# A two-layer decoder trunk on one core: reordering the chain of its post-norms and moving small operations between engines

## The chip, the core and the metric

The kernel runs on one core of a Trainium2 chip. The metric is the device time of one execution, in microseconds (us); less is better. Engines are named as in the profile: PE is TensorE (matrix products and 128x128 transposes), DVE is VectorE, ACT is ScalarE, POOL is GpSimd, SP is SyncE, which issues most DMAs.

## What is computed

The input is x, 512 tokens by 1024 channels in float32, and one condition vector c. Two layers follow each other; each has two sub-layers and each sub-layer ends in a post-norm. Cut to what matters here:

```python
for l in range(2):
    mod = silu(c) @ ada_w[l] + ada_b[l]          # 6 x 1024: shift, scale, gate, twice
    shift1, scale1, gate1, shift2, scale2, gate2 = split(mod, 6)
    h = x * (1 + scale1) + shift1
    a, u, v = split(h @ w_in[l])                 # 512 columns each
    y_a = pool_mixer(a, pool_w[l], pool_scale[l])         # windows 2, 4, 8, 16
    y_b = gelu(u) * (tril(sgu_w[l]) @ norm(gelu(v)) + sgu_b[l])
    x = layernorm(alpha * x + gate1 * (concat(y_a, y_b) @ w_out[l])) * ln1_g + ln1_b
    h = x * (1 + scale2) + shift2
    g, val = split(h @ w_up[l])                  # 2816 columns each
    f = (gelu(causal_conv3(g)) * val) @ w_down[l]
    x = layernorm(alpha * x + gate2 * f) * ln2_g + ln2_b
```

## The kernel before, in words

Every product is made of three float32r matmuls (high part by high part, high by low, low by high), so each weight tile is loaded by SP, cast to its high part `whi` on ACT (L178) and its low part `wlo` is subtracted on DVE (L181). The order of the work on every engine is the order of the program text; nothing is rescheduled. Generators stand for pieces of work that the text weaves between others (`weave`), and counters say how many weight tiles are loaded, split and ready; at most four stand ready at a norm.

Tokens lie in four chunks of 128 (`NCH`). The residual `xr[c]` is one tile of 128 tokens by 1024 channels for each chunk. A sub-layer ends in two projections, one for each half of the channels. `project` makes the first half for all chunks (banks `ps0`). Then `project_and_norm` (L404) goes chunk by chunk: the second half on PE (`n_pj`), on DVE the gated residual of that half (`residual`, L339 and L341 or L343), `bn_stats` of both halves (L428), `bn_aggr` (L320), on POOL the eps (L322) and the power -0.5 (L323), on DVE the normalisation in place (L434), on PE eight transposes of the normalised chunk (`turn`, L349), on ACT the affine map of the next sub-layer by columns (L361) and the high part `hh` (L363), on DVE the low part `hl` (L364). PE's order is: second half of chunk 0, of chunk 1, transposes of 0, second half of chunk 2, transposes of 1, second half of chunk 3, transposes of 2. `after_norm` (L483) goes on with four weight tiles of the next product over chunks 0 and 1; between its second and its third tile stand the transposes of chunk 3; then come the same four tiles over chunks 2 and 3. The low parts of up to four weight tiles are split around chunk 3: one ahead of its second half, the others behind its `bn_aggr`.

This chain occurs three times: behind the mixer of layer 0 (the first norm), behind the MLP of layer 0 (the second), behind the mixer of layer 1 (the third). The last norm, at the end, is `project_and_end` (L440), which shares `rstd_of` (L318). The residual of the following sub-layer is `xr * (alpha*g) + alpha*b`: ACT scales the rows g and b as soon as they are loaded (L378) and POOL computes it on whole chunks (`next_residuals`, L367).

The small loads of the mixer of layer 0 (`poolw`, `wst`, `sb`), the counts `rcnt`, the columns of layer 1 and four loads for the gating norm are issued by POOL at the very start (L227 to L233), on a DMA queue of its own. During layer 0 DVE also sums the modulation products (`ada_sum`, L243), a 128x1024 operation for each 512 KB of `ada_w`; the ones that the first norm needs end right ahead of it.

## Time and profile before

| what | value |
|---|---|
| time, median of 3 runs | 1016.14 us (1015.49 to 1018.05) |
| time of the profiled execution | 1017.41 us |
| its span, first to last instruction | 1015.7 us |
| PE busy | 986.6 us, 97% of the span |
| DVE busy | 648.1 us, 64% |
| ACT busy | 364.1 us, 36% |
| POOL busy | 108.5 us, 11% |

The profiled execution took 1.71 us more than its span, and 1.27 us more than the median. PE is busy nearly throughout, so the time is PE's work plus the holes in it. A row of a timeline gives the start of an instruction in us from the start of the span, its duration, engine, line, operation, what it writes and reads, its shape, and in brackets the idle time in front of it with what ended it. A row of a table by stretches gives the busy time of each engine, then the granted clock of PE (1.00 is 2.4 GHz, 0.50 is 1.2 GHz), the busy share of the 16 DMA engines and what they moved.

### The profile page before, as it was taken

To read this page: it belongs to the slowest core of one execution; us is meant where nothing else is said; L and a number is where in the kernel's file an instruction comes from. 1 tells how busy PE (TensorE), PEld (TensorE's weight loads), DVE (VectorE), ACT (ScalarE), POOL (GpSimd) and SP (SyncE) were. 2 spreads that over 40 slices of the span, in tenths; PEclk is the share of its full clock that TensorE was granted. 3 is DMA by queue.
4 is the path that set the end of the run, shared out by engine and by line. 5 is a ranking of instruction groups with operands and counts; after the bars stand their busy time and mean duration, and the time that the engine had idled before them with its cause. 6 is when DMAs were issued, how large, how long until landed. Compare 5 with 4: busy or idle time off the path is not lost.

```text
span 1015.7 us, 11993 instructions
## 1 busy us (share of the span) xinstructions
PE 986.6 (97%) x4691; PEld 826.9 (81%) x4691; DVE 648.1 (64%) x907; ACT 364.1 (36%) x532; POOL 108.5 (11%) x89
## 2 busy tenths in 40 slices
PE   6999979999999999999999999999999999999996
PEld 5788768888888888888888878888888888888885
DVE  5979986868644376585699455877544245444456
ACT  3553264443322233333263432733433213333300
POOL 2010028000000000000064100540000000000002
PEclk9999999999999999999999999999999999999999
DMA  9979514767632355476115221355323332323302
GB/s 323 406 296 352 194 57 145 245 198 243 193 121 86 142 182 191 154 242 207 42 63 181 100 69 36 104 197 179 121 87 101 104 104 83 103 86 102 125 1 83
DMA packets 43849, 153.55 MB, mean 151 GB/s; under 512 B 5152, under 2 KB 5312, under 8 KB 43792
## 3 DMA queue, kind: packets, MB, share of 16 engines
q1 hardware_dynamic: 43344, 151.89, 43.6%
q0 software_dynamic: 448, 0.89, 0.3%
q8 instruction: 37, 0.61, 0.3%
q14 instruction: 20, 0.16, 0.1%
HBM read 150.67 MB, written 2.10 MB: 150 GB/s over the span
## 4 chain that ended last, share of the span: by engine, by line
PE 83%; DVE 9%; DMA 3%; ACT 3%; issue 1%; POOL 1%; SPq 0%; DVEq 0%; POOLq 0%; ACTq 0%
PE up L217 15%; PE up L218 15%; PE up L216 15%; PE down L387 6%; PE down L388 6%; PE down L389 6%; DVE wlo L181 2%; PE n_pj L388 1%; PE n_pj L389 1%; PE n_pj L387 1%; DMA ada<-in_ada_w_dram 1%; PE v L580 1%; PE a L580 1%; DMA raw_w_in<-in_w_in_dram 1%; ACT ht_n L361 1%
## 5 line engine op out<-in xcount | busy, mean ns | idle before, releaser
L218 PE MATMUL up<-hh,wlo 128*128 128x512 f32 (+1 forms) x768 | 285.9, 372 | 2.4 <-DVE wlo L181 2.4
L217 PE MATMUL up<-hl,whi 128*128 128x512 f32 (+1 forms) x768 | 285.9, 372 | 1.8 <-DVE hl L364 1.8
L216 PE MATMUL up<-hh,whi 128*128 128x512 f32 (+1 forms) x768 | 286.6, 373 | 0.0
L181 DVE TENSOR_TENSOR wlo<-raw_w_up,whi 128x1024 fp32r<-128x1024 f32 x88 | 118.7, 1353 | 143.8 <-ACT whi L178 143.8
L218 PEld LDWEIGHTS up<-hh,wlo 128*128 128x128 f32 x768 | 145.2, 189 | 27.7 <-DVE wlo L181 2.8
L217 PEld LDWEIGHTS up<-hl,whi 128*128 128x128 f32 x768 | 145.3, 189 | 26.9 <-DVE hl L364 2.2
L216 PEld LDWEIGHTS up<-hh,whi 128*128 128x128 f32 x768 | 145.4, 189 | 25.0
L181 DVE TENSOR_TENSOR wlo<-raw_w_down,whi 128x1024 fp32r<-128x1024 f32 x44 | 53.9, 1225 | 114.9 <-ACT whi L178 113.3
L178 ACT CAST whi<-raw_w_up 128x1024 fp32r<-128x1024 f32 x88 | 90.9, 1045 | 57.0 <-PE down L389 52.6
L387 PE MATMUL down<-whi,gh 128*128 128x512 f32 x272 | 105.8, 389 | 0.0
L388 PE MATMUL down<-wlo,gh 128*128 128x512 f32 x272 | 105.8, 389 | 0.0
L389 PE MATMUL down<-whi,gl 128*128 128x512 f32 x272 | 105.8, 389 | 0.0
L243 DVE SCALAR_TENSOR_TENSOR ada<-ada,c 128x1024 f32<-128x1024 f32 x68 | 82.6, 1217 | 4.4 <-DMA ada<-in_ada_w_dram 4.4
L828 ACT ACTIVATE y<-y 128x512 f32<-128x512 f32 x44 | 27.9, 634 | 143.2 <-DVE y L825 143.2
L178 ACT CAST whi<-raw_w_down 128x1024 fp32r<-128x1024 f32 x44 | 46.1, 1048 | 80.6 <-PE down L389 80.6
L818 ACT ACTIVATE y<-up,cols 128x512 f32<-128x512 f32 x44 | 34.3, 779 | 89.5 <-PE up L218 87.9
L389 PEld LDWEIGHTS down<-whi,gl 128*128 128x128 f32 x272 | 51.1, 188 | 10.7
L387 PEld LDWEIGHTS down<-whi,gh 128*128 128x128 f32 x272 | 51.0, 188 | 10.6
L388 PEld LDWEIGHTS down<-wlo,gh 128*128 128x128 f32 x272 | 51.0, 188 | 10.6
L322 POOL TENSOR_SCALAR rs_n<-mv_n 128x1 f32<-128x1 f32 x12 | 7.2, 600 | 480.7 <-DVE mv_n L320 480.7
L361 ACT ACTIVATE ht_n<-tr_n,B,A 128x128 f32<-128x128 f32 x96 | 36.0, 454 | 60.1 <-PE tr_n L349 60.1
L181 DVE TENSOR_TENSOR wlo<-raw_w_in,whi 128x1024 fp32r<-128x1024 f32 (+1 forms) x26 | 37.8, 1477 | 10.0 <-ACT whi L178 9.9
(170 smaller groups left out, 1459.6 us busy)
## 6 DMA issues: line engine op xcount, KB each, us to landing
raw_w_up<-in_w_up_dram SPq DMA_DIRECT2D x88, 512.0 KB, 3.3
ada<-in_ada_w_dram SPq DMA_DIRECT2D x68, 512.0 KB, 4.2
raw_w_down<-in_w_down_dram SPq DMA_DIRECT2D x44, 512.0 KB, 3.2
raw_w_in<-in_w_in_dram SPq DMA_DIRECT2D x24, 512.0 KB, 5.5
raw_w_out<-in_w_out_dram SPq DMA_DIRECT2D x16, 512.0 KB, 4.5
xr<-in_ada_w_dram SPq DMA_DIRECT2D x12, 512.0 KB, 9.9
lent<-in_ada_w_dram SPq DMA_DIRECT2D x8, 512.0 KB, 9.9
lent_h<-in_ada_w_dram SPq DMA_DIRECT2D x8, 512.0 KB, 7.6
```

The lines of the kernel that those rows point to most:

```text
L178: A.copy(hi, src)
L181: (eng or V).tensor_tensor(lo, src, hi.bitcast(F32), op=ALU.subtract)
L216: T.matmul(ps, w[0], x[0], start=start, stop=False)
L217: T.matmul(ps, w[0], x[1], start=False, stop=False)
L218: T.matmul(ps, w[1], x[0], start=False, stop=stop)
L243: V.scalar_tensor_tensor(raw, raw, 0.5, c2, op0=ALU.mult, op1=ALU.mult, accum_out=modc[l][:, o : o + 1])
L361: A.activation(tmp[:, w], ps[hf][:, w], AF.Identity, bias=cb[:, k : k + 1], scale=ca[:, k : k + 1])
L387: T.matmul(ps[:, f], ah[:, cs], wh, start=i + j == 0, stop=False)
L388: T.matmul(ps[:, f], ah[:, cs], wl, start=False, stop=False)
L389: T.matmul(ps[:, f], al[:, cs], wh, start=False, stop=i + j == n - 1)
L818: A.activation(y, pg, AF.Identity, bias=col[:, C_CB + j : C_CB + j + 1], scale=col[:, cw + 2 : cw + 3])
L828: A.activation(y, y, AF.Gelu_apprx_tanh)
```

## The change

- The norm's chain: the first halves of chunks 0 and 1 (residual and statistics) come ahead of the loop, that of chunk c + 2 between the statistics and the normalisation of chunk c. The statistics of a half follow its residual at once. The low parts `hl` of chunk c - 1 come behind the normalisation of chunk c. Of the weight tiles split at chunk 3 two come ahead of its second half, one between its statistics and its normalisation, a fourth (in the first norm) behind.
- eps is added on DVE, the power stays on POOL.
- The next residuals are computed on DVE, one 128x1024 operation behind each pair of an MLP or each weight tile of the mixer, instead of on POOL; 8 operations behind each of the three norms.
- ACT scales the rows g and b behind the first two pairs of the MLP, not ahead of the last chunk's affine map.
- The nine small loads go to SP: `rcnt` behind the second group of first loads, the others behind five more modulation sums, where the mixer of layer 0 begins. `z_bias` of layer 0 moves behind `pool_group(3)`.

```diff
-    poolw, wst, sb = mix_loads(0, G)
-    G.dma_start(rcnt, a["rcnt"])
-    G.dma_start(cols[1], a["cols"][1])
...
+    def first_mix_loads():
+        tiles = mix_loads(0)
...
+                    nc.sync.dma_start(t[:, i, :], a[n][i].rearrange("(h d) -> d h", h=4))
+        nc.sync.dma_start(cols[1], a["cols"][1])
+        return tiles
...
-        G.tensor_scalar(rs, mv[:, 1:2], EPS, None, op0=ALU.add)
+        V.tensor_scalar(rs, mv[:, 1:2], EPS, None, op0=ALU.add)
         G.tensor_tensor(rs, rs, neg_half, op=ALU.pow)
...
     def next_residuals(grow, brow):
+
         for c in range(NCH):
-            G.tensor_tensor(xr[c], xr[c], grow, op=ALU.mult)
-            G.tensor_tensor(xr[c], xr[c], brow, op=ALU.add)
...
+            for row, op in ((grow, ALU.mult), (brow, ALU.add)):
+                later.append(lambda c=c, row=row, op=op: V.tensor_tensor(xr[c], xr[c], row, op=op))
+
+    def one_later():
+        if later:
+            later.pop(0)()
...
+        half(ps0[0], 0, 0)
+        half(ps0[1], 1, 0)
         for c in range(NCH):
...
             if c == NCH - 1:
-                refill(4 - len(ready), None, lows)
-                for f in lows[:1]:
-                    f()
-            before = None
-            if c:
-                before = modulate(c - 1, turn(c - 1, tag), tag, AB)
-            residual(ps, c, 1, gate, scale=scale)
-            for hf in range(2):
-                V.bn_stats(sts[c][:, hf, :], xr[c][:, halves(hf)])
+                split(2)
+            before = modulate(c - 1, turn(c - 1, tag), tag, AB) if c else None
+            half(ps, c, 1)
             mv, rs = rstd_of(sts[c], f"{tag}{c}")
-            for f in lows[1:]:
-                f()
-            if before:
-                next(before)
+            if c + 2 < NCH:
+                half(ps0[c + 2], c + 2, 0)
+            elif c == NCH - 1:
+                split(1)
             V.tensor_scalar(xr[c], xr[c], mv[:, 0:1], rs, op0=ALU.subtract, op1=ALU.mult)
             if before:
-                next(before)
-            if c + 1 < NCH:
-                residual(ps0[c + 1], c + 1, 0, gate, scale=scale)
+                weave([before])
+            if c == NCH - 1:
+                split(4)
...
+        if k == 1:
+            nc.sync.dma_start(rcnt, a["rcnt"])
...
-            pump(MIX_FILL[0], fill)
+            pump(MIX_FILL[0] - 1, fill)
+            poolw, wst, sb = first_mix_loads()
+            lower_triangles()
+            pump(1, fill)
...
                 weave([pair(0, *up[:2]), pair(1, *up[2:])], side * 4)
+                scaled((grow, brow))
...
                 weave([pair(j, *up)], side * 2)
                 j += 1
+                one_later()
```

Here `half` is `residual` and then `bn_stats` of one half, `split(n)` splits up to n weight tiles until four are ready, and `scaled` is ACT's scaling of the rows.

DVE at the start of the first norm, before: from the first half of chunk 0 (`res_0`, `xr_84`) to its normalisation by L434 and the first half of chunk 1 (`xr_85`).

```order
L339 TENSOR_TENSOR res_0_1058<-out_0_0_905,gate_2_722 128x512
L343 SCALAR_TENSOR_TENSOR xr_84<-xr_84,res_0_1058 128x512
L339 TENSOR_TENSOR res_1_1086<-n_0_pj_0_1061,gate_2_722 128x512
L343 SCALAR_TENSOR_TENSOR xr_84<-xr_84,res_1_1086 128x512
L428 BN_STATS stn_0_0_1054<-xr_84 128x6 x2
L320 BN_AGGR mv_n_0_0_1091<-stn_0_0_1054 128x2
L434 TENSOR_SCALAR xr_84<-xr_84,mv_n_0_0_1091,rs_n_0_0_1093 128x1024
L339 TENSOR_TENSOR res_0_1097<-out_0_1_906,gate_2_722 128x512
```

The same place now (the normalisation is L450; `xr_86` is chunk 2).

```order
L426 BN_STATS stn_0_0_1054<-xr_84 128x6
L340 TENSOR_TENSOR res_0_1062<-out_0_1_906,gate_2_720 128x512
L344 SCALAR_TENSOR_TENSOR xr_85<-xr_85,res_0_1062 128x512
L426 BN_STATS stn_0_1_1055<-xr_85 128x6
L340 TENSOR_TENSOR res_1_1091<-n_0_pj_0_1066,gate_2_720 128x512
L344 SCALAR_TENSOR_TENSOR xr_84<-xr_84,res_1_1091 128x512
L426 BN_STATS stn_0_0_1054<-xr_84 128x6
L321 BN_AGGR mv_n_0_0_1095<-stn_0_0_1054 128x2
L323 TENSOR_SCALAR rs_n_0_0_1097<-mv_n_0_0_1095 128x1
L340 TENSOR_TENSOR res_0_1100<-out_0_2_907,gate_2_720 128x512
L344 SCALAR_TENSOR_TENSOR xr_86<-xr_86,res_0_1100 128x512
L426 BN_STATS stn_0_2_1056<-xr_86 128x6
```

The first halves of chunks 1 and 2, three operations each, have moved ahead of the normalisation of chunk 0.

DVE at chunk 3 (`xr_87`) of the second norm, before.

```order
L339 TENSOR_TENSOR res_0_3912<-down_1_0_3_3555,gate_5_1882 128x512
L341 TENSOR_TENSOR xr_87<-res_0_3912,xr_87 128x512
L181 TENSOR_TENSOR wlo_3947<-raw_w_in_3680,whi_3946 128x1024
L339 TENSOR_TENSOR res_1_3968<-n_0_pj_3_3915,gate_5_1882 128x512
L341 TENSOR_TENSOR xr_87<-res_1_3968,xr_87 128x512
L428 BN_STATS stn_0_3_3728<-xr_87 128x6 x2
L320 BN_AGGR mv_n_0_3_3973<-stn_0_3_3728 128x2
L181 TENSOR_TENSOR wlo_3950<-raw_w_in_3713,whi_3949 128x1024
L181 TENSOR_TENSOR wlo_3953<-raw_w_in_3721,whi_3952 128x1024
L364 TENSOR_TENSOR hl_1042<-ht_n_0_2_0_3980,hh_1040 128x4x128
L434 TENSOR_SCALAR xr_87<-xr_87,mv_n_0_3_3973,rs_n_0_3_3975 128x1024
```

The same place now.

```order
L181 TENSOR_TENSOR wlo_3948<-raw_w_in_3680,whi_3947 128x1024
L181 TENSOR_TENSOR wlo_3951<-raw_w_in_3713,whi_3950 128x1024
L340 TENSOR_TENSOR res_1_3965<-n_0_pj_3_3916,gate_5_1877 128x512
L342 TENSOR_TENSOR xr_87<-res_1_3965,xr_87 128x512
L426 BN_STATS stn_0_3_3728<-xr_87 128x6
L321 BN_AGGR mv_n_0_3_3969<-stn_0_3_3728 128x2
L323 TENSOR_SCALAR rs_n_0_3_3971<-mv_n_0_3_3969 128x1
L181 TENSOR_TENSOR wlo_3975<-raw_w_in_3721,whi_3974 128x1024
L450 TENSOR_SCALAR xr_87<-xr_87,mv_n_0_3_3969,rs_n_0_3_3971 128x1024
```

The first half of chunk 3, one of its two statistics and an `hl` have gone from between the low parts and the normalisation.

SP where the mixer of layer 0 begins, now; before, `ada_82` follows `ada_81` at once.

```order
L82 DMA ada_81<-in_ada_w_dram 128x1024
L222 DMA poolw_551<-in_pool_w_dram 128x512
L223 DMA wst_552<-in_sgu_w_dram 128x512
L224 DMA sb_553<-in_sgu_b_dram 128x512
L232 DMA sgc<-in_sgu_ln_g_dram 128x4x1 x2
L232 DMA sbc<-in_sgu_ln_b_dram 128x4x1 x2
L233 DMA cols_97<-in_cols_dram 128x172
L82 DMA ada_82<-in_ada_w_dram 128x1024
```

Eight small loads now stand on SP's queue between two loads of `ada_w`.

## Rows read from the trace of the kernel before

**Rows 1.** Table by stretches: the first norm, and the MLP of layer 0 behind it.
```profile
118.00:165.00 47.00, 39.26 (x240) 33.74 (x239) 36.69 (x57) 24.47 (x49) 15.58 (x12) 1.00 0.23 79
165.00:495.00 330.00, 330.00 (x1498) 274.79 (x1498) 208.84 (x280) 107.07 (x133) 12.55 (x6) 1.00 0.54 179
```
**Rows 2.** Waits of PE from 118 to 165: us in total, times, longest.
```profile
PE tr_n L349 <- DVE xr L434: 2.9, 2, 2.2
PE up L218 <- DVE wlo L181: 2.4, 2, 1.7
PE up L217 <- DVE hl L364: 1.8, 2, 1.1
```
**Rows 3.** Timeline of PE at the first transposes of the first norm.
```profile
126.36 0.39 PE L389 MATMUL n_pj<-whi,ml 128*128 128x512 f32 x1
128.94 1.07 PE L349 MATMUL tr_n<-ident,xr 128*128 128x128 f32 x8 [2.19 <-DVE xr L434]
```
**Rows 4.** Timelines at chunk 3 of the second norm (519 on) and the third (646 on).
```profile
519.97 2.42 POOL L369 TENSOR_TENSOR xr<-xr,g 128x1024 f32<-128x1024 f32 x1
520.09 2.85 DVE L434 TENSOR_SCALAR xr<-xr,mv_n,rs_n 128x1024 f32<-128x1024 f32 x1
522.99 1.85 PE L349 MATMUL tr_n<-ident,xr 128*128 128x128 f32 x8 [2.19 <-DVE xr L434]
...
646.52 1.40 POOL L323 TENSOR_TENSOR rs_n<-rs_n,neg_half 128x1 f32<-128x1 f32 x1
...
648.88 1.47 PE L349 MATMUL tr_n<-ident,xr 128*128 128x128 f32 x8 [2.42 <-DVE xr L434]
```
**Rows 5.** Table by stretches behind those two holes.
```profile
523.00:527.00 4.00, 4.00 (x21) 4.00 (x22) 3.48 (x2) 2.94 (x8) 4.00 (x2) 0.57 0.06 23
650.00:652.00 2.00, 2.00 (x11) 2.00 (x10) 1.59 (x1) 1.79 (x4) 1.63 (x2) 0.50 0.94 379
```
**Rows 6.** Page, DMA queues: POOL's queue; packets, MB, share of 16 engines.
```profile
q0 software_dynamic: 448, 0.89, 0.3%
```
**Rows 7.** Table by stretches: the opening.
```profile
14.00:26.00 12.00, 10.68 (x36) 7.71 (x36) 9.76 (x17) 6.68 (x9) 0.00 (x0) 1.00 1.03 407
```
**Rows 8.** Timeline of PE: the last wait of the opening.
```profile
27.40 0.50 PE L218 MATMUL a<-hh,wlo 128*128 128x512 f32 x1 [0.53 <-DVE wlo L181]
```
**Rows 9.** Timelines of DVE and POOL at chunk 0 of the first norm.
```profile
122.80 0.68 DVE L339 TENSOR_TENSOR res<-out,gate 128x512 f32<-128x512 f32 x1
...
124.13 0.68 DVE L339 TENSOR_TENSOR res<-n_pj,gate 128x512 f32<-128x512 f32 x1
...
125.45 1.28 DVE L428 BATCH_NORM_STATS2 stn<-xr 128x6 f32<-128x512 f32 x2
...
127.38 0.56 POOL L323 TENSOR_TENSOR rs_n<-rs_n,neg_half 128x1 f32<-128x1 f32 x1
...
127.98 0.81 DVE L434 TENSOR_SCALAR xr<-xr,mv_n,rs_n 128x1024 f32<-128x1024 f32 x1 [1.00 <-POOL rs_n L323]
```
**Rows 10.** Timeline of DVE: a small operation.
```profile
122.23 0.17 DVE L310 TENSOR_SCALAR A<-modc 128x8 f32<-128x8 f32 x1
```
**Rows 11.** Timeline of PE: the first products, behind a hole.
```profile
14.28 0.79 PE L580 MATMUL v<-whi,hh 128*128 128x512 f32 x1 [5.22 <-ACT hh L526]
...
15.30 0.63 PE L580 MATMUL v<-whi,hh 128*128 128x512 f32 x1
15.72 0.63 PE L580 MATMUL v<-wlo,hh 128*128 128x512 f32 x1
```
**Rows 12.** Page, costliest groups: a 128x1024 operation with two inputs on DVE.
```profile
L181 DVE TENSOR_TENSOR wlo<-raw_w_down,whi 128x1024 fp32r<-128x1024 f32 x44 | 53.9, 1225 | 114.9 <-ACT whi L178 113.3
```
**Rows 13.** Timelines of DVE and POOL at the end.
```profile
1009.09 1.28 DVE L328 SCALAR_TENSOR_TENSOR xr<-xr,mv_end,g 128x1024 f32<-128x1024 f32 x1
1009.14 1.31 POOL L322 TENSOR_SCALAR rs_end<-mv_end 128x1 f32<-128x1 f32 x1 [4.37 <-DVE mv_end L320]
...
1011.13 1.41 DVE L331 SCALAR_TENSOR_TENSOR xr<-xr,rs_end,b 128x512 f32<-128x512 f32 x2 [0.76 <-POOL rs_end L323]
```

More of the change, by code (lines that the diff above doesn't have):

```diff
@@ L105, in trunk @@
     nc.sync.dma_start(cols[0], a["cols"][0])
+    rcnt = const.tile([P, 16], F32, name="rcnt")
     ident = const.tile([P, P], F32, name="ident")
@@ L218, in mm3, with mix_loads @@
         T.matmul(ps, w[1], x[0], start=False, stop=stop)
-    def mix_loads(l, eng):
+    def mix_loads(l):
         tiles = [unit(f"{n}{l}") for n in ("poolw", "wst", "sb")]
-        eng.dma_start(tiles[0], a["pool_w"][l])
-        eng.dma_start(tiles[1], a["sgu_w"][l])
-        eng.dma_start(tiles[2], a["sgu_b"][l : l + 1, :].partition_broadcast(P))
-        return tiles
-    poolw, wst, sb = mix_loads(0, G)
-    G.dma_start(rcnt, a["rcnt"])
-    G.dma_start(cols[1], a["cols"][1])
-    with nc.allow_non_contiguous_dma(reason="columns of the gating norm"):
-        for t, n in ((sgc, "sgu_ln_g"), (sbc, "sgu_ln_b")):
-            for i in range(L):
-                G.dma_start(t[:, i, :], a[n][i].rearrange("(h d) -> d h", h=4))
+        nc.sync.dma_start(tiles[0], a["pool_w"][l])
+        nc.sync.dma_start(tiles[1], a["sgu_w"][l])
+        nc.sync.dma_start(tiles[2], a["sgu_b"][l : l + 1, :].partition_broadcast(P))
+        return tiles
+    def first_mix_loads():
+        tiles = mix_loads(0)
+        with nc.allow_non_contiguous_dma(reason="columns of the gating norm"):
+            for t, n in ((sgc, "sgu_ln_g"), (sbc, "sgu_ln_b")):
+                for i in range(L):
+                    nc.sync.dma_start(t[:, i, :], a[n][i].rearrange("(h d) -> d h", h=4))
+        nc.sync.dma_start(cols[1], a["cols"][1])
+        return tiles
     ada = [(0, v) for v in (2, 4, 3, 5)] + [(1, v) for v in (1, 0, 2, 4, 3, 5)]
@@ L365, in modulate, with norm_rows @@
             yield
+    later = []
     def next_residuals(grow, brow):
         for c in range(NCH):
-            G.tensor_tensor(xr[c], xr[c], grow, op=ALU.mult)
-            G.tensor_tensor(xr[c], xr[c], brow, op=ALU.add)
-    def norm_rows(l, which, scale):
+            for row, op in ((grow, ALU.mult), (brow, ALU.add)):
[3 more added lines that the diff above has]
+            later.pop(0)()
+    def norm_rows(l, which):
         g = rows.tile([P, D], F32, tag="nrow", name=f"g{which}{l}")
@@ L376, in norm_rows, with scaled @@
             nc.sync.dma_start(t, a[f"ln{which}_{n}"][l : l + 1, :].partition_broadcast(P))
-            if scale:
-                A.activation(t, t, AF.Copy, scale=ALPHA)
         return g, b
+    def scaled(ts):
+        for t in ts:
+            A.activation(t, t, AF.Copy, scale=ALPHA)
+        return ts
     def pair_mms(ps, c, w, act, i, n, f=slice(0, HALF)):
@@ L410, in project_and_norm, with half, split @@
         sts = [small.tile([P, 2, 6], F32, tag="st2", name=f"st{tag}{c}") for c in range(NCH)]
-        residual(ps0[0], 0, 0, gate, scale=scale)
+        lows = []
+        def half(ps, c, hf):
+            residual(ps, c, hf, gate, scale=scale)
+            V.bn_stats(sts[c][:, hf, :], xr[c][:, halves(hf)])
+        def split(n):
+            refill(min(n, 4 - len(ready)), None, lows)
+            while lows:
+                lows.pop(0)()
+        half(ps0[0], 0, 0)
+        half(ps0[1], 1, 0)
         for c in range(NCH):
@@ L610, in trunk @@
             refill(3)
+            poolw, wst, sb = mix_loads(l)
             next_residuals(grow2, brow2)
-        if l:
-            poolw, wst, sb = mix_loads(l, nc.sync)
         at = []
@@ L721, in step, with lower_triangles @@
             return [g for g in gens if next(g, 0) is None]
-        w3 = wst.rearrange("p (h t) -> p h t", h=4)
-        G.affine_select(
-            out=w3, in_=w3, pattern=[[0, 4], [1, P]], compare_op=ALU.is_ge, fill=0.0, base=0, channel_multiplier=-1
-        )
+        def lower_triangles():
+            w3 = wst.rearrange("p (h t) -> p h t", h=4)
+            G.affine_select(
+                out=w3, in_=w3, pattern=[[0, 4], [1, P]], compare_op=ALU.is_ge, fill=0.0, base=0, channel_multiplier=-1
+            )
         if l:
+            lower_triangles()
             v_ps = [bank(f"v{l}_{c}") for c in range(NCH)]
@@ L758, in trunk @@
             norms = step(norms)
-            zbias = z_bias()
-            next(zbias)
             u_gelu(0, ps)
@@ L768, in trunk @@
             ps = u_tile(2)
+            zbias = z_bias()
+            next(zbias)
             pms = step([pool_mix(0), pool_mix(1)])
             u_gelu(2, ps)
+            pool_group(3)
             next(zbias, 0)
-            pool_group(3)
             refill(1)
@@ L854, in trunk @@
                 j += 1
+                one_later()
             if s == 1:
-                grow2, brow2 = norm_rows(l, 2, more)
+                grow2, brow2 = norm_rows(l, 2)
+                if more:
+                    later.append(lambda: scaled((grow2, brow2)))
             def after_down(i):
+                one_later()
                 refill(1)
```

6 lines of the change are left out of this document (3 added, 3 removed).

## The prediction

> **What bounds the kernel now.** The table by stretches comes first, because it shows where PE is not busy. In the MLP of layer 0 PE is busy 330.00 of 330 us, with 1498 matmul rows, 0.22 us from one start to the next; in the first norm, 118 to 165, it is busy 39.26 of 47 us [rows 1]. So the time is PE's work, and only holes in PE's row can be won. The waits of PE say what ends the holes of the first norm: normalised chunks (2.9 us), low parts of weights (2.4) and low parts of activations (1.8), all made by DVE [rows 2]. That is 7.1 us in six holes. The timeline shows that a hole costs a little more than its idle time: a matmul row lasts 0.39 us, though the next would start 0.22 us behind it. From 126.36 to 128.94 are 2.58 us, less 0.22 is 2.36 lost, for 2.19 of idle time [rows 3]. With 0.17 for each of the six, the first norm loses 8.1 us.
>
> The second and third norms have one hole each, both in front of the transposes of chunk 3: 2.19 and 2.42 us of idle time [rows 4], 2.36 and 2.59 lost. Behind them comes a second loss: the granted clock falls to the level of 1.2 GHz for a while. It is 0.57 of full speed in the four us behind the second norm's hole [rows 5], so (1 - 0.57) x 4 = 1.7 us of work are lost there; behind the third it is 0.50 over two us and more [rows 5], and I take 1.7 again. In the first norm no fall follows its 2.19 us hole: the clock is 1.00 over the whole stretch [rows 1].
>
> What remains is the opening, where PE waits for loads, and the tail behind the last product. Away from these five places PE has no holes to give.
>
> **The change, part by part.** All numbers are for the profiled execution, 1017.41 us, span 1015.7; the median of the runs is 1.27 us lower, and I subtract the same sum from it.
>
> *Opening.* POOL's queue moves 0.89 MB, 0.3% of the DMA engines' time in the span, all at the start [rows 6]. The engines are full there: share 1.03 and 407 GB/s from 14 to 26 us [rows 7]. PE's last wait of the opening ends at 27.40, on a low part of a weight that has just been loaded [rows 8]; from there PE runs without a hole until the first norm, so what the loads before 27.40 gain, PE gains. Taking the 0.89 MB out of the front is worth 0.89 / 0.407 = 2.2 us by bytes and 0.3% of 1015.7 = 3.0 by engine time. I take 2.6, as neither row is nearer. In their new place the eight loads stand on SP ahead of an `ada_w` load and of the weights of the output projection; POOL's mask waits for `wst`, and four small POOL operations of the gating norm queue behind the mask. I cost that at nothing, because DVE has the modulation sums to do meanwhile; if that cover is gone, the price is at most the loads' own 3.0 us.
>
> The Trainium skill, "DMA: Bandwidth & Descriptors", section "Issuing engines are not separate DMA queues", says that DMAs of all issuing engines share the same 16 engines and interleave, so that another issuer saves only issue time. By it the move from POOL to SyncE is worth 0 in itself and the sum would be 9.6; only the later place can pay.
>
> *First norm.* DVE is late here: it starts the first half of chunk 0 at 122.80, when PE has long finished it, and normalises chunk 0 at 127.98 [rows 9]. A half costs 1.33 us (122.80 to 124.13) and its statistics 0.64 (1.28 for two), together 1.97 [rows 9]. The new order puts the first halves of chunks 1 and 2 ahead of that normalisation, 3.9 us more; in return the wait of 1.00 us for POOL goes [rows 9], since the power of 0.56 us runs beside chunk 2's half, while eps costs DVE about 0.2 (a small operation, 0.17 [rows 10]). The first transposes come 3.9 - 1.0 + 0.1 = 3.0 us later: the first hole grows from 2.36 to 5.4 us. I expect PE to be slow behind it: behind the one hole of such a length, 5.22 us, the first eight products start some 0.42 us apart instead of 0.22 [rows 11], 1.6 us lost. The granted clock reads 1.00 there [rows 7], so it stays open whether that is the clock; behind the holes of the second and third norms it is, for 1.7. I take 1.7. The other five holes close. From then on the first halves are done early; the low parts of two weights stand ahead of chunk 3's second half; ACT's scaling of the rows no longer stands in front of the last affine map, whose low parts PE waited for. So 8.1 becomes 5.4 + 1.7 = 7.1: 1.0 won. Upper bound: PE at full pace, 2.7. Lower bound: the two waits for weights (2.4 + 0.34) stay, 1.7 lost.
>
> *Second norm.* The normalisation of chunk 3 takes 2.85 us here, against 0.81 in the first norm; it starts 0.12 us behind a POOL operation of 2.42 us on the next residuals [rows 4, 9]. With these on DVE and later, it takes 0.81. It also starts earlier: the first half of chunk 3 (1.33) and one statistic (0.64) no longer stand in front of it, so at 520.09 - 2.0 = 518.1 and it ends at 518.9, while PE is ready at 522.99 - 2.19 = 520.8. The hole closes with 1.9 us to spare, and the clock has no reason to fall: 2.36 + 1.7 = 4.1 won. Lower bound 2.36, if the clock falls all the same.
>
> *Third norm.* Here the normalisation waited for the power, which POOL ran beside a DVE operation in 1.40 us and ended at 647.92 [rows 4], against 0.56 alone [rows 9]. Two us earlier it starts at 645.9 and ends at 646.7; PE is ready at 648.88 - 2.42 = 646.5 [rows 4]. A hole of 0.2 stays, and I expect no fall behind it, since none followed the 2.19 of the first norm: 2.59 + 1.7 - 0.2 = 4.1 won. Lower bound 2.4, with a fall.
>
> *Next residuals.* 24 operations of 1.23 us (the same form in [rows 12]) are 29 us more on DVE. Eight of them, 10 us, fall into the MLP of layer 0, where DVE is busy 208.84 of 330 us [rows 1]; up to four weights stand ready ahead of PE. I cost them at nothing; without that cover each would cost its 1.23.
>
> *Tail.* eps takes POOL 1.31 us at 1009.14, beside DVE's own operation of 1.28 [rows 13]. On DVE it takes 0.2, so by these rows alone 1.1 would be won. But the power now runs beside that same DVE operation, and beside DVE it took 1.40 [rows 4]: 1009.09 + 0.2 + 1.40 + 0.1 = 1010.8 against 1011.13 [rows 13]. I take 0.35, between 0 and 1.1.
>
> The skill's "GPSIMD Engine Reference", section "8. Key points", has a rule against this part: GpSimd shares its SBUF interfaces with VectorE and contends with its instructions of two SBUF inputs, which that operation is. By the rule the power stays slow there and the sum is 12.2; without it 12.9. The trace agrees, with the 1.40.
>
> *Sum:* 2.6 + 1.0 + 4.1 + 4.1 + 0.35 = 12.2 us. The profiled execution would come to 1005.2, the median to 1016.14 - 12.2 = **1003.9**. Low ends: 2.2 - 1.7 + 2.36 + 2.4 + 0 = 5.3, so 1010.8; high ends: 3.0 + 2.7 + 4.1 + 4.3 + 1.1 = 15.2, so 1000.9.
>
> **Rivals.** *The opening gains nothing.* POOL's packets may only have filled time that SP's queue could not use. For it: PE's first wait, of 5.22 us, ends on ACT, not on a load [rows 11]. Against it: a share of 1.03. This leaves 9.6 won: 1006.5. The DMA rule above would give this if the place did not matter.
>
> *The low parts still hold chunk 3.* One of them still stands between statistics and normalisation, and the power beside it is slow. If the second and third holes and their falls of the clock stay, 4.0 is left: 1012.1. Against it: 1.9 us to spare in the second norm. For it: 0.2 us missing in the third.
>
> *DVE becomes the bound (slower).* Each of the 24 added operations stands ahead of a low part. If the weights ready ahead of PE ran out, each would hold PE for 1.23 us: 29 lost, 17 net, 1033. It decides once DVE needs more time for a pair of weight tiles than PE; with 209 + 10 of 330 us it is far from that [rows 1].
>
> *The edit does not do what it says:* POOL would still run next residuals or the statistics stand where they stood. The order of the instructions excludes it, so it has no chance of its own.
>
> **How the numbers follow.** The forecast, with its own bounds, gets 0.72; the opening without gain 0.14; the low parts 0.08; DVE as the bound 0.03; mixtures near no change 0.03. The first two together lie between 1000.9 and 1010.8; 8 in 10 need less of the upper end, so 1000.5 to 1009. A change of under 0.3%, 3 us, cannot be told from none: faster takes the first three cases, most of 0.94, I say 0.92; same 0.04; slower 0.04.
>
> **What would show it.** Right: POOL has no 128x1024 operation left; the second norm's transposes of chunk 3 follow without a hole and the clock stays at 1.00 there; PE's wait at 27.40 comes near 25; the first norm has one hole, of 5 us, with products 0.42 us apart behind it. Wrong: waits of PE for `wlo` in the MLPs; holes left in front of chunk 3; an opening as long as before. A first norm without the long hole would mean that DVE is not as late as I read it.

## The result, and the profile after

The changed kernel takes 1004.83 us (median of four, 1004.31 to 1005.96) against 1016.48 for the kernel before beside it: a ratio of 0.9885, 95% interval 0.9868 to 0.9903. The prediction was 1003.9. The profiled execution took 1004.31, span 1002.3; that of before 1017.41, span 1015.7. So the two spans lie 13.4 us apart, the medians 11.65.

The page of the changed kernel, busy time and DMA queues:

```profile
PE 983.6 (98%) x4691; PEld 824.9 (82%) x4691; DVE 646.8 (65%) x947; ACT 363.6 (36%) x532; POOL 25.0 (2%) x40
...
q1 hardware_dynamic: 46176, 152.78, 44.3%
```

POOL fell from 108.5 to 25.0 us, and its DMA queue, 0.89 MB before [rows 6], is gone. DVE took 24 operations of 1.22 us more and is busy no longer than before (646.8 for 648.1). So about 29 us of its busy time before was not work of its own; the experiments below show that it came with POOL's operations.

Table by stretches, columns as in [rows 1]: the first norm, the MLP behind it, and the places of the second and third norm's holes:

```profile
118.00:165.00 47.00, 41.39 (x273) 37.85 (x272) 33.67 (x57) 23.00 (x47) 3.13 (x4) 0.96 0.32 107
165.00:495.00 330.00, 330.00 (x1481) 273.96 (x1480) 217.15 (x297) 109.33 (x138) 0.55 (x1) 1.00 0.53 174
515.00:519.00 4.00, 4.00 (x37) 4.00 (x36) 0.99 (x2) 3.00 (x8) 0.00 (x0) 1.00 0.09 32
637.00:641.00 4.00, 3.98 (x35) 3.78 (x34) 2.24 (x4) 2.88 (x8) 0.00 (x0) 1.00 0.72 276
```

The last two answer to [rows 5]: there PE stood at 0.57 and 0.50 of full speed, here it is busy (4.00 and 3.98 of 4 us) at 1.00. In the first stretch PE has one wait left, where [rows 2] had three kinds. First the waits of PE from 118 to 165, then PE's timeline around that wait:

```profile
PE tr_n L350 <- DVE xr L450: 5.6, 1, 5.6
```

```profile
122.74 0.39 PE L400 MATMUL n_pj<-whi,ml 128*128 128x512 f32 x1
128.72 1.94 PE L350 MATMUL tr_n<-ident,xr 128*128 128x128 f32 x8 [5.59 <-DVE xr L450]
...
131.62 0.39 PE L398 MATMUL n_pj<-whi,mh 128*128 128x512 f32 x1
```

This is the hole of [rows 3], grown from 2.36 to 5.75 (128.72 less 122.74, less the 0.23 in which the next would have started). The granted clock behind it, in the table by stretches below, is 0.51 and 0.64 over four us. PE itself was idle in the first 0.72 of them, so the loss is better taken from the starts: from the first transpose to the fourth product behind the transposes are 2.90 us (128.72 to 131.62). In the kernel before they are 1.60 (128.94 [rows 3] to 130.54), at a clock of 1.00. So 1.3 us are lost. The row of the kernel before, then the clock of the changed kernel:

```profile
130.54 0.40 PE L387 MATMUL n_pj<-whi,mh 128*128 128x512 f32 x1
```

```profile
128.00:130.00 2.00, 1.28 (x6) 1.31 (x7) 1.93 (x4) 0.11 (x1) 0.00 (x0) 0.51 0.00 0
130.00:132.00 2.00, 2.00 (x9) 1.72 (x8) 1.90 (x5) 1.97 (x6) 0.55 (x1) 0.64 0.00 0
```

The openings: PE's first product and its last wait for a low part, which answer to [rows 11] and [rows 8]. They come 3.36 and 3.85 us earlier.

```profile
10.92 0.80 PE L598 MATMUL v<-whi,hh 128*128 128x512 f32 x1 [1.86 <-ACT hh L544]
...
23.55 0.50 PE L218 MATMUL a<-hh,wlo 128*128 128x512 f32 x1 [0.31 <-DVE wlo L181]
```

DVE, then PE at chunk 3 of the second norm, which answers to [rows 4]: the normalisation takes 0.81 for 2.85 and is done at 514.09; PE gets to the transposes at 515.33, with no idle time in front: 1.24 us to spare.

```profile
511.53 0.15 DVE L323 TENSOR_SCALAR rs_n<-mv_n 128x1 f32<-128x1 f32 x1
511.61 1.23 DVE L181 TENSOR_TENSOR wlo<-raw_w_in,whi 128x1024 fp32r<-128x1024 f32 x1
513.28 0.81 DVE L450 TENSOR_SCALAR xr<-xr,mv_n,rs_n 128x1024 f32<-128x1024 f32 x1 [0.44 <-POOL rs_n L324]
```

```profile
515.33 1.04 PE L350 MATMUL tr_n<-ident,xr 128*128 128x128 f32 x8
```

**Where the time went.** All kernels of this table issue the same 4691 products and transposes, so the start of the same one in two traces, subtracted, gives what a stretch won (minus) or lost. Taken ahead of the first norm (122 us in the trace of before), behind each of the first three norms (330, 545, 700) and at PE's end, with the rest of the span as the tail:

| profiled execution, against before | opening | first norm | second | third | tail | sum |
|---|---|---|---|---|---|---|
| predicted | -2.6 | -1.0 | -4.1 | -4.1 | -0.35 | -12.2 |
| the changed kernel | -3.62 | -1.70 | -3.96 | -3.74 | -0.41 | -13.43 |
| a1, loads alone | -3.22 | +0.22 | -0.03 | +3.25 | -0.14 | +0.09 |
| a2, residuals alone | +0.16 | -2.49 | -3.61 | -0.10 | 0.00 | -6.04 |
| a3, order alone | +0.24 | +2.69 | +0.09 | -2.97 | -0.01 | +0.04 |
| c1, changed, residuals on POOL | -3.34 | +2.55 | +0.01 | -2.85 | -0.40 | -4.02 |

### The profile page after: what moved, and what is told of

Same layout as the page of the kernel before. It is cut to its first block, busy times and chain, and to the rows that moved or that the text cites. A ratio compares the mean times of both kernels' runs of the same rounds, so it can differ in the third digit from the quotient of the medians.

```text
span 1002.3 us, 11962 instructions
## 1 busy us (share of the span) xinstructions
PE 983.6 (98%) x4691; PEld 824.9 (82%) x4691; DVE 646.8 (65%) x947; ACT 363.6 (36%) x532; POOL 25.0 (2%) x40
## 4 chain that ended last, share of the span: by engine, by line
PE 90%; DVE 7%; ACT 1%; issue 1%; DMA 1%; SPq 0%; POOLq 0%; DVEq 0%
PE up L218 16%; PE up L217 16%; PE up L216 16%; PE down L400 6%; PE down L399 6%; PE down L398 6%; PE n_pj L398 2%; PE n_pj L399 2%; PE n_pj L400 2%; DVE wlo L181 1%; PE tr_n L350 1%; PE v L598 1%; PE a L598 1%; PE end L400 1%; PE end L399 1%; PE end L398 1%
## 5 line engine op out<-in xcount | busy, mean ns | idle before, releaser
L181 DVE TENSOR_TENSOR wlo<-raw_w_up,whi 128x1024 fp32r<-128x1024 f32 x88 | 107.3, 1223 | 150.4 <-ACT whi L178 150.4
L856 ACT CAST gh<-y 128x512 fp32r<-128x512 f32 x44 | 27.3, 620 | 43.0 <-DVE y L854 43.0
L854 DVE TENSOR_TENSOR y<-y,up 128x512 f32<-128x512 f32 x44 | 30.0, 685 | 18.0 <-PE up L218 14.2
```

Of the source, the lines that this page charges most:

```text
L181: (eng or V).tensor_tensor(lo, src, hi.bitcast(F32), op=ALU.subtract)
L854: V.tensor_tensor(y, y, pv, op=ALU.mult)
```

## The experiments

**The parts alone (a1, a2, a3), and the loads early on SyncE (b3).** The forecast added its terms as if each were its own. a1 keeps of the change only the loads, the mask and the place of `z_bias`; a2 only the next residuals and the scaling of the rows; a3 only the order.

```diff
# a1, a2: project_and_norm as before; a1, a3: next_residuals and norm_rows as before; a2, a3: loads as before
-        V.tensor_scalar(rs, mv[:, 1:2], EPS, None, op0=ALU.add)
+        G.tensor_scalar(rs, mv[:, 1:2], EPS, None, op0=ALU.add)
```

> The kernel before with the loads alone moved (the row of counts early on SyncE, the eight small loads late on SyncE, the mask and the bias of the gating norm behind them); norm, residuals and eps as before. Theory, the opening pays by itself: PE's first product comes 3.4 us and its last wait of the opening 3.6 to 3.9 us earlier than in the kernel before (14.28 and 27.40 there, 10.92 and 23.55 in the changed one), all later holes stay as they are, and the time falls by 3.6 us, to 1012.9. Rival, VectorE is late in the first norm anyway and takes the gain back: the first hole of the norm grows by what the opening gave, and under 1 us is won. The on-record estimate was 2.6.

Measured: 1016.08 against 1017.0, ratio 0.9993 (0.9984 to 1.0002): nothing. Both theories miss. The opening does pay, 3.22, and PE keeps it for 500 us. It is lost in the third norm, whose hole grows from 2.58 to 4.97. POOL and DVE at that place:

```profile
645.19 2.41 POOL L370 TENSOR_TENSOR xr<-xr,g 128x1024 f32<-128x1024 f32 x1 [1.10 <-ACT g L379]
```

```profile
644.71 0.69 DVE L365 TENSOR_TENSOR hl<-ht_n,hh 128x512 fp32r<-128x512 f32 x1
645.32 2.84 DVE L435 TENSOR_SCALAR xr<-xr,mv_n,rs_n 128x1024 f32<-128x1024 f32 x1
648.08 2.84 DVE L365 TENSOR_TENSOR hl<-ht_n,hh 128x512 fp32r<-128x512 f32 x1
```

POOL's operation on the next residuals starts 0.13 us ahead of the normalisation of chunk 3, and this takes 2.84. In the kernel before, POOL's started 0.39 us behind the normalisation there (648.41 and 648.02), and this took 0.81: the third norm was spared by 0.39 us what the second norm had. In both kernels POOL's start waits for ACT's scaling of the row g. Counted from `bn_aggr`, POOL starts 0.17 us earlier in a1 (3.18 for 3.35) and the normalisation 0.35 later (3.31 for 2.96). Why a shorter opening moves these tenths is not shown; the median, no better than before, speaks for the same loss in most executions.

> The kernel before with the next residuals alone moved to VectorE and spread (with the rows scaled later); loads, order of the norm and eps as before. Theory, POOL's 128x1024 operations make the second norm's hole and the order of the chain makes the third's: the normalisation of chunk 3 falls from 2.85 to about 0.8 us in the second norm, its hole from 2.35 to under 0.5 and the fall of the clock goes (3.5 to 4 won); in the third norm the power still runs beside a low part, and hole and fall stay (2.6 + 1.7); in the first norm the two waits behind chunk 3 (0.92 + 1.27) shrink, 0 to 2 won. 1010.5 to 1013. Rival, the order of the chain makes both holes: under 2 won. Rival, both holes come from POOL: 8 won or more.

Measured: 1011.37 against 1017.0, ratio 0.9946 (0.9933 to 0.9958), 5.6 won. The theory holds, place by place: second norm -3.61, third -0.10, first -2.49 (the two waits behind its chunk 3 are gone; I had given them 0 to 2). DVE in the second norm, then PE, POOL and DVE in the third:

```profile
517.76 0.81 DVE L444 TENSOR_SCALAR xr<-xr,mv_n,rs_n 128x1024 f32<-128x1024 f32 x1
```

```profile
642.94 1.97 PE L349 MATMUL tr_n<-ident,xr 128*128 128x128 f32 x8 [2.42 <-DVE xr L444]
```

```profile
640.58 1.40 POOL L323 TENSOR_TENSOR rs_n<-rs_n,neg_half 128x1 f32<-128x1 f32 x1
```

```profile
639.25 2.31 DVE L181 TENSOR_TENSOR wlo<-raw_w_up,whi 128x1024 fp32r<-128x1024 f32 x2
641.48 0.68 DVE L364 TENSOR_TENSOR hl<-ht_n,hh 128x512 fp32r<-128x512 f32 x1
642.08 0.81 DVE L444 TENSOR_SCALAR xr<-xr,mv_n,rs_n 128x1024 f32<-128x1024 f32 x1
```

In the second norm the old order is good enough once POOL is silent: the normalisation starts 2.96 us behind `bn_aggr` (514.80), as before (517.13 to 520.09), and only its length has changed. In the third the old order still keeps the hole: DVE goes from `bn_aggr` (639.12) over two low parts of weights and one `hl` to the normalisation (642.08) without idle time. The power beside them, slow as it is (1.40), is done at 641.98, so it is not the first thing to blame.

> The kernel before with the new order of the norm's chain alone (first halves early, low parts around the last chunk); loads, residuals and eps stay on POOL as before. Theory: the chain of chunk 3 starts 2 us earlier in the second and third norm; POOL's next residuals follow the power and so start 2 us earlier too, so the normalisation still takes 2 to 3 us where they meet it; the hole of the second norm shrinks from 2.35 to about 0.3, that of the third from 2.58 to between 0 and 2; the first norm has one long hole of 5 to 6 us with a fall of the clock and keeps slow low parts behind chunk 3. 5 to 8 won, 1008.5 to 1011.5. Rival, without the residuals moved the order is worth nothing in the second norm: hole and fall stay there, 2 to 4 won.

Measured: 1017.45 against 1017.0, ratio 1.0004 (0.9995 to 1.0012): nothing, against 5 to 8 that I expected. What I said of POOL following the power came true, and cost more than I said. The chain comes earlier, the hole of the second norm shrinks to 0.99 without a fall of the clock, and then the low parts of chunk 3 run beside POOL. DVE, second norm:

```profile
521.62 2.88 DVE L439 TENSOR_SCALAR xr<-xr,mv_n,rs_n 128x1024 f32<-128x1024 f32 x1 [0.76 <-POOL rs_n L323]
524.42 11.27 DVE L364 TENSOR_TENSOR hl<-ht_n,hh 128x512 fp32r<-128x512 f32 x4
535.61 3.42 DVE L181 TENSOR_TENSOR wlo<-raw_w_in,whi 128x1024 fp32r<-128x1024 f32 x1
```

Four low parts take 11.27 us, 2.8 each, where one takes 0.69 alone. PE waits for them:

```profile
532.95 0.39 PE L217 MATMUL in<-hl,whi 128*128 128x256 f32 x1 [1.43 <-DVE hl L364]
...
535.74 0.38 PE L217 MATMUL in<-hl,whi 128*128 128x256 f32 x1 [1.09 <-DVE hl L364]
```

So as long as POOL has the residuals, the order wins 2.97 in the third norm, loses 0.09 in the second and 2.69 in the first. With order and residuals together, in the changed kernel, the three norms win 3.74, 3.96 and 1.70. No run has the residuals and the loads without the order.

> The changed kernel with its small loads issued by SyncE at the place where POOL issued them before (ahead of the weights of the opening), all else as changed. Theory, the place decides and not the issuer: the same bytes stand in front again, PE's last wait of the opening comes back to 27 us, and 3 to 4 us are lost against the changed kernel: 1008.4. Rival, the issuer decides (POOL's own queue was what cost): the opening stays as short as in the changed kernel, 1004.8. A third outcome, over 1010: SyncE's queue holds the weights of the opening behind the small loads, which POOL's queue did not.

```diff
+    poolw, wst, sb = first_mix_loads()      # ahead of the first weights; rcnt behind it
...
-            poolw, wst, sb = first_mix_loads()
```

Measured: 1009.58, ratio 0.9933 (0.9919 to 0.9946) to before, 4.75 over the changed kernel. The first product comes at 15.99, later than with POOL's queue (14.28), and the opening loses 1.34 against before. The place decides, as the theory has it, and SyncE in front is worse than POOL in front, as the third outcome has it: its row of issues has the first `ada_w` load at 7.13 us instead of 1.70, behind nine small ones.

```profile
6.65 0.43 SPq L238 DMA_DIRECT2D rcnt<-in_rcnt_dram  x1
7.13 0.43 SPq L82 DMA_DIRECT2D ada<-in_ada_w_dram  x1
```

**The residuals back on POOL, the loads late on POOL, and two tries at the first norm and the opening (c1, a4, b1, b2).**

```diff
-            for row, op in ((grow, ALU.mult), (brow, ALU.add)):
-                later.append(lambda c=c, row=row, op=op: V.tensor_tensor(xr[c], xr[c], row, op=op))
...
+            G.tensor_tensor(xr[c], xr[c], grow, op=ALU.mult)
+            G.tensor_tensor(xr[c], xr[c], brow, op=ALU.add)
```

> The changed kernel with the next residuals back on POOL (and the rows scaled early again); the new places of the loads, the new order of the norm and eps on VectorE stay. The loads alone gave 3.2 us up to the third norm and lost them there; the order alone gave nothing: it lost 2.9 in the first norm, won 3 in the second, lost 3 again behind it (two waits of PE for low parts of 1.59 and 1.25, each of which took 2.8 us beside POOL instead of 0.69) and won 3.6 in the third. Theory, POOL's operations take the gains of the other parts back wherever they meet VectorE: 3 to 5 won against the kernel before, 1012 to 1014, with waits of PE for low parts of chunk 3 behind all three norms. Rival, each part brings what it brings in the changed kernel, and the residuals are worth only their own 5.6: 1010.4. Rival, nothing is left: 1016.

Measured: 1013.09 against 1016.53, ratio 0.9963 (0.9948 to 0.9978): 3.4 won, as the theory has it. Without the move of the 24 operations (and the later scaling of the rows that goes with it) 8.3 of the 11.65 are gone (1013.09 - 1004.83). In the second norm the normalisation is early (517.80) and slow (2.88), and the low parts take 11.27 again:

```profile
517.80 2.88 DVE L440 TENSOR_SCALAR xr<-xr,mv_n,rs_n 128x1024 f32<-128x1024 f32 x1 [0.44 <-POOL rs_n L324]
520.61 11.27 DVE L365 TENSOR_TENSOR hl<-ht_n,hh 128x512 fp32r<-128x512 f32 x4
```

```diff
-        nc.sync.dma_start(tiles[0], a["pool_w"][l])
+        (nc.sync if l else G).dma_start(tiles[0], a["pool_w"][l])      # so all of first_mix_loads
```

> The changed kernel with its seven late small loads issued by POOL at the same late place (the row of counts stays early on SyncE). Theory, the place decides: the opening stays as short as in the changed kernel (first product at 10.9, last wait at 23.6), and the time is 1004.8, within 1.5. Rival, the issuer matters: loads on POOL's queue land later or take more of the DMA engines, the mask comes late and PE waits in the gating norm: 1006 to 1008.

Measured: 1007.99, ratio 0.9914 (0.99 to 0.9929): 3.2 over the changed kernel. My theory fails, and the rival's time is right for another reason. POOL, the opening:

```profile
1.50 0.75 POOL L222 DMA_DIRECT2D poolw<-in_pool_w_dram  x1
...
6.30 0.55 POOL L233 DMA_DIRECT2D cols<-in_cols_dram  x1
```

A late place in the program is a late time only on a queue that has something to do. POOL has nothing ahead of these loads, so it issues them from 1.50 us on, and the first product comes at 14.01. What the change needs is SyncE's row of waiting loads in front of them.

```diff
-        half(ps0[0], 0, 0)
-        half(ps0[1], 1, 0)
+        ahead = 2 if scale is None else 1
+        for c in range(ahead):
+            half(ps0[c], c, 0)
...
-            if c + 2 < NCH:
-                half(ps0[c + 2], c + 2, 0)
+            if c + ahead < NCH:
+                half(ps0[c + ahead], c + ahead, 0)
```

> The changed kernel, but in the first norm alone the first halves run one chunk ahead instead of two, so one half (2.05 us) stands behind the normalisation of chunk 0 instead of ahead of it. Theory, VectorE is the bound from the modulation sums to the end of the first norm, and the order only moves the hole: the first hole shrinks from 5.75 to 3.7, one of 0.5 to 1 us opens ahead of chunk 1, and waits for low parts or the last chunk of 1 to 2 us come back; 0 to 1 won: 1003.8 to 1004.8. Rival, the first hole is lost time by itself: 2 won, and 1.7 more if the fall of the clock goes: 1001 to 1003.

Measured: 1003.59, ratio 0.9872 (0.9858 to 0.9887), 1.2 under the changed kernel, 0.96 by the profiled executions; the two intervals overlap, so whether it is faster is not shown. The hole is 3.74 and the clock falls all the same; 0.48 and 0.42 open at chunk 3. Mostly the theory: DVE has no rest between its modulation sums and about 133 us, so a hole that is closed early opens late.

```diff
-AHEAD, N_IDLE = 2, (5, 20)
+AHEAD, N_IDLE = 2, (5, 30)
```

> The changed kernel with ten more idle products in the opening (30 for 20), which fill PE's hole of 1.86 us ahead of the first product. The first ten products start 0.43 us apart there instead of 0.23, about 2 us. Theory, the opening is bound by loads: the next wait of PE, at 18.19 for a low part, and the one at 23.55 end where they ended, whatever PE's pace before them; 0 won, 1004.8. Rival, PE's pace counts: the products start 0.23 apart from the first on and 1 to 2 us are won: 1003 to 1004.

Measured: 1005.82, ratio 0.9888 (0.9871 to 0.9904), 1.0 over the changed kernel, again with overlapping intervals. The idle products did not change the pace: the first eight products still start 0.43 apart, 0.7 us later. Neither theory was tried by it, since the pace did not move. The rest of the loss in the profiled execution is in the first norm, by a longer fall of the clock (below).

**Products into the first norm's hole (e1, e2, f1).** If DVE is late for chunk 0, PE can multiply chunk 2 meanwhile. e1 does this in the first norm alone; e2 also normalises chunks 1 and 2 on ACT; f1 shifts two low parts on DVE.

```diff
+        p2 = product(2)
+        t0 = turn(0, tag)
+        p3 = product(3)
+        t1 = turn(1, tag)
+        second(p2, 2)
+        weave([modulate(0, t0, tag, AB)])
+        normal(2)
+        t2 = turn(2, tag)
...
+                A.activation(xr[c], xr[c], AF.Identity, bias=nb, scale=rs)      # e2, chunks 1 and 2
...
+        next(g0)
+        normal(2)
+        weave([g0])      # f1, and so for chunk 3
```

> The changed kernel, but in the first norm alone PE multiplies chunk 2 before the transposes of chunk 0, and chunk 3 before those of chunk 1, so that products fill the hole of 5.75 us; the first halves stay two chunks ahead, and the low parts of activations stand later on VectorE. Theory, VectorE is the bound of the first norm: chunk 0 is normalised at 128.6 as before, chunk 2's product ends at 128.2, so the first hole goes and with it the fall of the clock (7.4 us there), but VectorE's own work up to the normalisation of chunk 3 ends at about 146.5 against 149.5, so holes of 3 to 4 us in all open ahead of the transposes of chunks 2 and 3: 2 to 4 won against the changed kernel, 1001 to 1003. Rival, PE's order is the bound: the whole 7.4 is won, 997.5. Rival, the place of the hole makes no difference: 1004.8.

> The same, with the normalisation of chunks 1 and 2 in the first norm on ScalarE, which has nothing to do there until the first transposes; VectorE keeps one operation of 128x1 for each (0.15 us) in place of 0.8. Theory, VectorE is the bound: 1.3 us more are won than by the order of the products alone, 1000 to 1002. Rival, the way over ScalarE (one of its operations of 1024 columns takes about 1.05 us, and it waits for VectorE's small one) makes the chain of a chunk longer by as much: no difference to the order alone.

e1 measured: 1001.57, ratio to before 0.9846 (0.9831 to 0.9861), 3.3 under the changed kernel: the best version here. The theory holds. PE of e1:

```profile
128.45 1.06 PE L350 MATMUL tr_n<-ident,xr 128*128 128x128 f32 x8 [0.17 <-DVE xr L482]
134.83 1.03 PE L350 MATMUL tr_n<-ident,xr 128*128 128x128 f32 x8
138.02 1.09 PE L350 MATMUL tr_n<-ident,xr 128*128 128x128 f32 x8 [2.15 <-DVE xr L482]
```

The hole of 5.75 is gone, one of 2.32 stands ahead of chunk 2, and DVE's normalisation of chunk 3 ends at 146.33, close to the 146.5 I had added up. The first norm wins 4.04 against before, where the changed kernel won 1.70.

e2 measured: 1007.72, ratio 0.9908 (0.9892 to 0.9925), 6.2 over e1. Both expectations miss. ACT:

```profile
133.24 1.25 ACT L486 ACTIVATE xr<-xr,nb_n,rs_n 128x1024 f32<-128x1024 f32 x1 [25.12 <-DVE nb_n L485]
134.39 1.48 ACT L362 ACTIVATE ht_n<-tr_n,B,A 128x128 f32<-128x128 f32 x4
```

ACT takes its instructions in order: the affine map of chunk 0, whose transposes ended at about 130, stands behind the normalisation of chunk 1, which waits until 133.24 for DVE. So ACT idled while it had work, DVE waited for ACT's `hh` (6.6 us in all), and PE waited 4.5 us for chunk 2. An engine with free time is no help to a chain if its own work must queue behind that chain.

> The version with products ahead of transposes, and in the first norm two small moves on VectorE: only the first half of chunk 0's low parts (0.64 us) stands ahead of the normalisation of chunk 2, and the low part of the third weight (1.2) stands behind the normalisation of chunk 3 instead of ahead of it, with half of chunk 2's low parts covering POOL's power. Theory, VectorE's order decides when the last two transposes start: those of chunk 2 come 0.6 us earlier (137.4 for 138.0) and those of chunk 3 1.0 to 1.5 us earlier (146.98 there), 1 to 1.5 won against that version, 1000 to 1000.6. Rival, the fall of the clock behind the hole ahead of chunk 2 holds PE whatever VectorE does: 0 to 0.5 won, 1001 to 1001.6.

Measured: 1002.72, ratio 0.9863 (0.9848 to 0.988), 1.15 over e1 with overlapping intervals. Nothing won, as the rival has it for the hole and the fall (2.25 us ahead of chunk 2, clock 0.84 and 0.73 in the eight us behind it); 1.37 for 0.77 open at the first low parts. About 0.6 of the rest is the opening, which differs by that much between executions of code that is the same there.

**eps back on POOL (g1).**

> The changed kernel with eps back on POOL, all else as changed. Theory, eps on VectorE is needed for the third norm more than for the tail: beside VectorE the addition takes POOL 1.1 to 1.3 us and the power follows it, so the normalisation of chunk 3 comes 0.5 to 0.9 us later in each norm; the third norm has only about 0.1 us to spare (chunk 3 is normalised at 637.34, its transposes start at 637.40), so a hole of 0.5 to 0.9 us opens there, without a fall of the clock; the tail gets 0.26 longer (2.08 us from the last statistics to the last operation, 2.34 before). 0.8 to 1.2 lost: 1005.6 to 1006. Rival, only the tail moves: 0.3 lost, 1005.1. Rival, the new hole takes the clock down again: 2.5 to 3 lost, 1007.5.

Measured: 1005.65, ratio 0.9895 (0.9878 to 0.9911), 0.8 over the changed kernel, with overlapping intervals: the time is the theory's, its reason isn't, since no hole opens in the third norm beyond the changed kernel's. POOL and DVE in the third norm:

```profile
635.88 1.09 POOL L323 TENSOR_SCALAR rs_n<-mv_n 128x1 f32<-128x1 f32 x1 [7.05 <-DVE mv_n L321]
637.06 0.57 POOL L324 TENSOR_TENSOR rs_n<-rs_n,neg_half 128x1 f32<-128x1 f32 x1
```

```profile
637.66 0.81 DVE L450 TENSOR_SCALAR xr<-xr,mv_n,rs_n 128x1024 f32<-128x1024 f32 x1 [0.76 <-POOL rs_n L324]
```

From the start of `bn_aggr` to the normalisation are 2.07 us here (635.59 to 637.66) and 1.99 in the changed kernel (634.54 to 636.53). Whichever of the two small operations falls beside DVE's low part takes 1.1 to 1.5; the other takes its time alone (0.57 for the power here). So eps on DVE is worth 0.08 in a norm, and 0.27 in the tail (2.35 for 2.08 there). Most of the rest lies in the first norm, which wins 0.44 against before here and 1.70 in the changed kernel: its fall of the clock lasts longer. Whether eps has to do with that stays open. The changed kernel's own four executions lie as far apart (1004.31 and 1004.32 at a mean clock of 0.996, 1005.34 and 1005.96 at 0.994), so a fall of either length may belong to the same code; only one of the four has a trace.

## Why the prediction was right

**The sum.** 12.2 forecast, 13.4 between the profiles, 11.65 between the medians. The range held it. It came so near in part because misses cancel: against the profiles the opening and the first norm won 1.7 more than forecast, the second and third norm 0.5 less. The medians are nearer than the profiles because the one of before was above its median and the one after at the bottom of its runs.

**Opening, 2.6 forecast, 3.62 found.** Right in kind, too small. By bytes 2.2, by engine time 3.0; a1 alone gives 3.22, and code that is the same there differs by 0.6 from one execution to the next (3.29 in f1, 3.91 in e1). The rival "the opening gains nothing" falls with a1. By the rule of the Trainium skill ("DMA: Bandwidth & Descriptors", section "Issuing engines are not separate DMA queues") the issuer was worth 0 but for the time of issuing, and the forecast left only the place to pay. b3 and a4 agree with that 0, since neither SyncE in front (15.99) nor POOL at a late line (14.01) gets the first product to 10.92; the time of issuing was not small in b3 (7.13 for 1.70). But "later place" in my text meant the line in the program; a4 shows that it has to be the time of issue.

**First norm, 1.0 forecast, 1.70 found.** The steps came, with other sizes: the hole grew by 3.4 (5.75 for 2.36; 3.0 forecast), the slow pace behind it cost 1.3 (1.7 forecast), and the other five holes gave back 6.4 (5.7 forecast); 6.4 - 3.4 - 1.3 = 1.7. That a fall of the clock came was partly luck: I had inferred it from the slow first products of the opening, and these are slow in b2 behind 0.42 us of idle time too, so a long hole is not what makes them slow. What the forecast did not see is that the order does not pay in this norm. Residuals and scaling alone (a2) win 2.49 here, in the two waits behind chunk 3; the order alone (a3) loses 2.69; and beside the residuals it still costs about 0.8 (1.70 for 2.49), since 3.4 and 1.3 stand against 3.9 from the other three holes. For the last two waits I named ACT's scaling of the rows alone. It is there: in the kernel before the affine map of chunk 3 starts at 157.00, behind the scaling, and in a2 at 153.27. But POOL has a share that I left out: the two low parts behind it took 1.01 and 1.76 before, and 4.74 together in c1, for 0.69 each alone. No run scales early without POOL's residuals, so the two shares are not told apart.

**Second norm, 4.1 forecast, 3.96 found.** The size is right, and the first reason given (0.81 for 2.85) is nearly the whole of it: residuals alone win 3.61, the order alone loses 0.09. "It also starts earlier" is worth 0.35 beside that, and 1.24 us are to spare for 1.9 forecast, since the normalisation waits 0.44 for a power of 1.42 that was left out there.

**Third norm, 4.1 forecast, 3.74 found.** Here the order is the cause, as forecast: alone it wins 2.97, the residuals alone 0.10. The hole of 0.2 that the forecast left is there: 0.3 us lie between the last product's start and the transposes (637.10 to 637.40), where the next would have started 0.12 behind it, and the normalisation ends at 637.34. The clock gives back 1.55 for 1.7, and 0.2 is lost at the transposes of an earlier chunk, at 617.8. One reading was wrong: in the kernel before the normalisation did not wait for the power. Its row has no idle time in front; DVE works on two low parts and an `hl` up to it, and the power ends at 647.92, 0.1 us before it starts. DVE there:

```profile
645.19 2.31 DVE L181 TENSOR_TENSOR wlo<-raw_w_up,whi 128x1024 fp32r<-128x1024 f32 x2
647.42 0.68 DVE L364 TENSOR_TENSOR hl<-ht_n,hh 128x512 fp32r<-128x512 f32 x1
648.02 0.81 DVE L434 TENSOR_SCALAR xr<-xr,mv_n,rs_n 128x1024 f32<-128x1024 f32 x1
```

So what the order took out of the way is one low part and the `hl`, besides the first half and a statistic. Only now does the normalisation wait for the power: 0.44 us, for 1.48 beside the one low part that is left.

**Next residuals at nothing.** Right: PE is busy 330.00 of 330 us in that MLP, with DVE at 217.15 where 208.84 + 10 was forecast. The rival of a bound DVE falls with that. What the forecast did not have is that DVE's busy time in total would not grow. POOL's operations had cost DVE about as much as they now cost on DVE: 24 x 1.22 = 29 us more work, and 1 us less busy time; in a2, where nothing else of DVE's changed, 29 us more work and 6.5 less busy time (641.6 for 648.1).

**Tail, 0.35 forecast, 0.41 found.** From the row of the last `bn_aggr` to the last operation 2.08 for 2.34, so 0.26; the power beside DVE took 1.45, as [rows 4] had shown with 1.40. The rule of the Trainium skill on GpSimd's interfaces ("GPSIMD Engine Reference", section "8. Key points") would have it so too, since that DVE operation has two SBUF inputs.

**What the sum hid.** The forecast gave each part its own gain. Right for the whole, it would have been wrong for the loads or the order shipped alone: the loads alone win nothing clear of noise of their 3.2, the order alone nothing. The term that carried the change, the residuals, stood in my text at nothing for itself and inside the second norm for its use; in the first norm, where it won most of what was won, only the scaling of the rows was named.

## What to carry to other kernels

Work on an idle engine is not free if it slows the busy one: read what the other engine's same instruction takes with and without it (0.69 and 2.8 here), and price the pair. A gain ahead of such a meeting can vanish at the meeting, so measure parts together as well as alone. Where a chain is late, let the waiting engine do later work that is ready (e1) before moving the chain to an engine whose queue holds its own next step (e2).

## What the runs showed that I had not expected

- A DVE operation that starts just behind one of POOL's 128x1024 operations took about POOL's time whatever its own size: 0.69 became 2.8 (four in 11.27), 0.81 became 2.84 to 2.88, 1.22 became 3.42. Two that started late in POOL's operation, in the first norm before, took less: 1.01 and 1.76 for 0.69.
- The fall of the clock does not follow from a hole's length alone. 2.35 us in the kernel before's first norm had none, 2.32 in e1 had one. Behind holes of the same 5.6 to 5.8 us the granted clock over 126 to 136 us was 0.83 in the changed kernel and 0.66 in g1 and b2, where the first norm won 1.3 us less (0.44 and 0.39 for 1.70). Why stays open. The changed kernel, then g1, then b2:

```profile
126.00:136.00 10.00, 7.28 (x31) 6.30 (x32) 8.75 (x15) 4.16 (x10) 0.99 (x2) 0.83 0.00 0
```

```profile
126.00:136.00 10.00, 7.47 (x25) 6.32 (x26) 8.40 (x14) 4.15 (x10) 1.34 (x3) 0.66 0.00 0
```

```profile
126.00:136.00 10.00, 6.60 (x22) 5.60 (x23) 9.36 (x18) 4.15 (x10) 1.10 (x2) 0.66 0.00 0
```

- In the opening products start 0.43 apart for 3.6 to 4 us while the granted clock reads 1.00, behind 5.22 us of idle time [rows 11], 1.86 (the changed kernel) and 0.42 (b2) alike. PE of b2:

```profile
11.61 0.79 PE L598 MATMUL v<-whi,hh 128*128 128x512 f32 x1 [0.42 <-ACT hh L544]
12.20 0.63 PE L598 MATMUL v<-wlo,hh 128*128 128x512 f32 x1
12.62 0.63 PE L598 MATMUL v<-whi,hh 128*128 128x512 f32 x1
```
